# A two-layer trunk with grouped experts: scattered rows inside the weight stream, three experts by selection, modulation on TensorE, and another order around the overflow loop

## Chip, cores and metric

One core of a Trainium2 chip. The metric is the time of one execution in device microseconds (us); lower is better. "Before" is the median of three runs.

## What is computed

A trunk of two layers over 512 tokens of width 1024, all in float32. Each layer takes a modulation from a condition vector, mixes tokens (layer 0 with a chunkwise matrix memory, layer 1 with differential attention), then routes every token to 2 of 16 experts of one group. Cut to what matters:

```python
for l in range(2):
    mod = silu(c) @ w_ada[l] + b_ada[l]                # 1024 -> 6 * 1024
    sh1, sc1, g1, sh2, sc2, g2 = split(mod, 6)
    h = rms(x, norm1[l]) * (1 + sc1) + sh1
    x = x + g1 * mixer[l](h)                           # layer 0: mLSTM, layer 1: attention
    h = rms(x, norm2[l]) * (1 + sc2) + sh2
    # every token: its best group of 4 experts, the best 2 in it, normed weights
    y = sum over its 2 experts of weight * ((silu(h @ w_gate) * (h @ w_up)) @ w_down)
    x = x + g2 * y
```

## The kernel before

**Start.** `load` (lines 209 to 216) asks for a chunk on SP's queue. `ada_half` (272 to 296) makes half of shift and scale of layer 0: for each of the two, two chunks of 4 x 128 rows by 512 columns; ScalarE and VectorE multiply each row block by its scalar of silu(c) and add them up in `acc`; `column_sums` (259 to 265) turns the result with TensorE and reduces it on VectorE. `modulated` (359 to 364) then makes the operand of the first projection, `proj_cols` (424 to 437). The second half, `rest_of_h` (491 to 496), runs between the first products. All products of the large matrices are triples: a weight is split by `split` (218 to 223) into a high part (ScalarE) and a low part (VectorE, for some POOL), and `triple` (225 to 230) multiplies high by high, low by high, high by low.

**Routing.** `route` (974 to 1176) gives `tile_done` (1009): per 128 tokens, POOL multiplies the token rows, ScalarE takes the square sum, `rstd_of` (317) makes the root on POOL; `logits` (1032), `choose` (1046) and `place` (1071) follow with tiny VectorE instructions. `order` (1107) ranks the 13 experts of varying size by their counts and finds how many blocks overflow (`past`); `by_rank` (1137) sorts row numbers and weights by rank; `weigh` (1152) makes the weights. Then `overflow` (1455 to 1476), a loop over overflow blocks with a count known only at run time: every engine reads `past` and passes the loop's entry and exit.

**Experts.** `moe` (1239 to 1577) takes 16 experts in turn: 9 with 128 tokens in triples, the last 7 (`few`) with 64 tokens in plain float32, TensorE holding 64 columns of tokens, the weights moving, two halves side by side. An expert is 6 parts of 1 MB: 4 gate-up, 2 down. `sequence` (1207) gives their order, `Prefetch` (1227) asks for them into 15 buffers, each as an earlier part is used up. Results go back in two ways. Most experts write theirs, weighted, with an indirect transfer into a table of 1024 rows in memory (`keep`, `keep_few`, 1312). The last two (`NSEL`) are added by selection: a 0/1 matrix (`places`, 1322) multiplies the weighted result (`weighted_few`, 1306) into the 512 tokens (`to_tokens`, 1329); their table rows are filled with zero rows at expert 1. Near the end `scattered_rows` (1478 to 1490) reads the table back in eight transfers of 512 KB into buffers of the splits, and `combine` (1492 to 1497) adds the two rows of each token, multiplies by the modulation row and adds to the tokens: three VectorE instructions per 128 tokens. `keep_in_program_order` (`ordered`) fixes the order of these instructions, and TensorE's of the last experts, as written; a scheduler sets the rest.

In the last expert: `combine((0,))` ahead of the activation, (1, 2) behind it, (3) behind the down product; then the selection products and an addition for each half of each 128 tokens, and in layer 1 the transfers out.

## Time and profile before

| | |
|---|---|
| median of 3 runs | 1259.03 us (1256.88 to 1259.57) |
| profiled execution, its own time | 1258.35 us |
| its span, first to last instruction | 1256.4 us |
| TensorE busy, share | 1113.8 us, 89% |
| VectorE, ScalarE, POOL busy | 70%, 56%, 30% |
| mean granted TensorE clock | 0.932 |
| moved | 320.79 MB, mean 255 GB/s |

Times in the rows count from the span's start. A busy share is an average over stages of different kinds: layer 0 has its mixer up to about 250 us, routing to 320, experts to 590; layer 1 its mixer to 950, routing to 978, experts to the end. PE is TensorE, DVE VectorE, ACT ScalarE, POOL GpSimd, SP the engine that asks for transfers. "[x <-y]" behind a row is the idle time of its engine before it and what ended that. The granted clock is 1.00 at 2.4 GHz and 0.50 at 1.2 GHz.

### The profile page before, as it was taken

What the parts mean: (1) busy time and instruction counts of PE and PEld (TensorE: products, weight loads), DVE (VectorE), ACT (ScalarE), POOL (GpSimd) and SP (SyncE); (2) the same over time, 40 slices, a digit from 0 to 9 for tenths busy, and PEclk for the clock granted to TensorE, in tenths of its full rate; (3) what the DMA queues carried; (4) which work ended last, traced back from release to release, by engine and by line L of the source; (5) the groups of instructions that cost most, each with busy time, mean ns of one, the idle gap of its engine ahead of it and who ended that gap; (6) DMA issues with size and microseconds to landing.
All of it is one profiled execution on the core that took longest, in us unless ns stands there. A gap on an engine that the chain in (4) does not pass through costs nothing. (4 is left out here: it accounts for less than half of the span.)

```text
span 1256.4 us, 16914 instructions
## 1 busy us (share of the span) xinstructions
PE 1113.8 (89%) x5714; PEld 816.6 (65%) x5714; DVE 873.6 (70%) x1622; ACT 698.2 (56%) x1164; POOL 381.4 (30%) x273
## 2 busy tenths in 40 slices
PE   3899999987899999995799999888897999999994
PEld 2577877766777875332688877665576787875331
DVE  6955878887788994006767889795776798993006
ACT  5456675442788884112656666565552788884110
POOL 2544572452211111102351455551332211101100
PEclk7799999997899999998799999897896899999997
DMA  9777662183899999998233335320464799999995
GB/s 349 248 246 282 243 233 101 66 341 143 289 390 383 377 390 365 397 409 272 94 102 117 119 127 175 131 73 1 168 248 167 268 386 375 387 384 366 391 410 202
DMA packets 105196, 320.79 MB, mean 255 GB/s; under 512 B 12674, under 2 KB 25098, under 8 KB 105105
## 3 DMA queue, kind: packets, MB, share of 16 engines
q1 hardware_dynamic: 96272, 298.67, 64.6%
q0 software_dynamic: 8832, 20.99, 4.6%
q8 instruction: 47, 0.77, 0.2%
q14 instruction: 45, 0.36, 0.1%
HBM read 309.66 MB, written 20.45 MB: 263 GB/s over the span
## 5 line engine op out<-in xcount | busy, mean ns | idle before, releaser
L253 POOL TENSOR_TENSOR acc<-acc,ada 128x1024 f32<-128x1024 f32 x58 | 151.0, 2604 | 89.4 <-ACT ada L252 36.7
L1275 PE MATMUL pge<-we,xfe 128*64 128x512 f32 x448 | 103.2, 599 | 2.5 <-DMA we<-in_moe_w_gu_dram 2.5
L1247 POOL DMA_INDIRECT xg<-h2d,lstd x26 | 26.4, 1016 | 235.8 <-PE xTe L380 156.3
L1284 DVE TENSOR_TENSOR acte<-acte,pge 128x256 f32<-128x256 f32 x14 | 5.9, 420 | 125.0 <-ACT acte L1283 125.0
L252 ACT ACTIVATE ada<-ada,cact 128x1024 f32<-128x1024 f32 x58 | 64.7, 1143 | 30.8 <-DMA ada<-in_w_ada_dram 30.7
L1275 PEld LDWEIGHTS pge<-we,xfe 128*64 128x64 f32 x448 | 29.3, 136 | 55.6 <-issue 48.2
L877 ACT ACTIVATE p<-p,mx 128x128 f32<-128x128 f32 (+3 forms) x64 | 35.6, 557 | 42.5 <-DVE mx L876 42.5
L1302 PE MATMUL pye<-we,aTe 128*64 128x512 f32 x224 | 54.1, 624 | 1.7 <-ACT aTe L1291 1.1
L320 POOL TENSOR_TENSOR qrs<-qrs,nhalf 128x4 f32<-128x4 f32 x32 | 36.7, 1151 | 61.2 <-DVE qrs L319 47.8
L870 PE MATMUL s<-kTb,qTb 64*128 64x128 f32 (+3 forms) x128 | 44.8, 530 | 11.1 <-DVE mx L873 10.4
L465 POOL TENSOR_TENSOR wo<-wo,grow 128x1024 f32<-128x1024 f32 x16 | 40.1, 2523 | 30.2 <-DVE wos102l L222 15.1
L1302 PEld LDWEIGHTS pye<-we,aTe 128*64 128x64 f32 x224 | 16.4, 144 | 36.5 <-issue 31.9
L873 DVE CUSTOM_DVE_ANT_0 p<-s,maskW 128x128 f32<-128x128 f32 (+3 forms) x64 | 29.8, 484 | 12.6 <-PE s L870 5.5
L1283 ACT ACTIVATE acte<-pge 128x256 f32<-128x256 f32 x14 | 5.4, 384 | 54.6 <-PE pge L1275 54.6
L1333 PE MATMUL pcf<-yo,self 64*128 64x512 f32 x64 | 18.9, 636 | 17.6 <-DVE acte L1284 15.9
L1314 ACT ACTIVATE yo<-pye,twins 128x512 f32<-128x512 f32 x10 | 6.9, 687 | 48.7 <-PE pye L1302 48.7
L1315 POOL DMA_INDIRECT yd<-yo,rows x10 | 10.0, 998 | 78.1 <-ACT yo L1314 77.5
L844 DVE TENSOR_TENSOR qrow<-qrow,qrs 128x256 f32<-128x256 f32 x32 | 26.5, 828 | 7.9 <-POOL qrs L320 7.6
L1291 ACT ACTIVATE aTe<-aTe 128x256 f32<-128x256 f32 x14 | 5.4, 383 | 45.5 <-PE aTe L1289 45.5
L1398 POOL DMA_INDIRECT yd<-yoe,lstd x12 | 14.7, 1225 | 52.4 <-ACT yoe L1503 50.7
L320 POOL TENSOR_TENSOR ors<-ors,nhalf 128x2 f32<-128x2 f32 (+1 forms) x12 | 12.0, 999 | 58.9 <-DVE ors L319 25.0
L250 DVE SCALAR_TENSOR_TENSOR acc<-ada,cact,acc 128x1024 f32<-128x1024 f32 x12 | 15.4, 1281 | 19.4 <-POOL acc L253 16.5
(2545 smaller groups left out, 3963.2 us busy)
## 6 DMA issues: line engine op xcount, KB each, us to landing
we<-in_moe_w_gu_dram SPq DMA_DIRECT2D x128, 1024.0 KB, 9.4
we<-in_moe_w_down_dram SPq DMA_DIRECT2D x64, 1024.0 KB, 10.5
ada<-in_w_ada_dram SPq DMA_DIRECT2D x48, 1024.0 KB, 5.2
yk<-yd SPq DMA_DIRECT2D x16, 512.0 KB, 10.0
wo<-in_a_w_out_dram SPq DMA_DIRECT2D x4, 1024.0 KB, 4.9
wo<-in_b_w_out_dram SPq DMA_DIRECT2D x4, 1024.0 KB, 6.2
x<-in_x_dram SPq DMA_DIRECT2D x4, 512.0 KB, 5.2
qk0w<-in_a_w_in_dram SPq DMA_DIRECT2D x2, 1024.0 KB
```

The costliest lines, as they stand in the source:

```text
L252: A.activation(raw[:, k], raw[:, k], AF.Copy, scale=cact[:, kt:kt + 1])
L253: G.tensor_tensor(acc, acc, raw[:, k], op=ALU.add)
L320: G.tensor_tensor(r, r, nhalf[:, 0:ncol], op=ALU.pow)
L465: G.tensor_tensor(raw[:, k], raw[:, k], grow, op=ALU.mult)
L844: V.tensor_tensor(row3, row3, r[:, :, None].to_broadcast([P, ng, BHD]), op=ALU.mult)
L870: T.matmul(ps[:, 0:n], part(qTs, h)[q0:q0 + BHD, j * P:(j + 1) * P], part(kTs, h)[q0:q0 + BHD, 0:n], start=True, stop=True)
L873: V.tensor_tensor_reduce(p[:, 0:n], ps[:, 0:n], maskW[:, S - n:S], scale=1.0, scalar=NEG, op0=ALU.add, op1=ALU.max, accum_out=mx[:, cc:cc ...
L877: A.activation(p[:, 0:n], p[:, 0:n], AF.Exp, scale=0.125, bias=mx[:, cc:cc + 1], accum_out=mx[:, 2 + cc:3 + cc])
L1247: G.indirect_dma_start(out=xg[0:n], out_offset=None, in_=h2d[:, :], in_offset=bass.IndirectOffsetOnAxis(ap=itok[0:n], axis=0), bounds_chec ...
L1275: T.matmul(pgu[hf * CS:(hf + 1) * CS].rearrange("p (g c) -> p g c", g=2), x[:, kt], w[:, :, hf], start=kt == 0, stop=kt == NK - 1))
L1302: T.matmul(py[hf * CS:(hf + 1) * CS], aT[:, k, ch * CS:(ch + 1) * CS], w[:, 0, hf * 512:(hf + 1) * 512], start=ch + k == 0, stop=ch + k == 2))
L1333: ordered(T.matmul(banks[hf], sel[at, t], yo[at], start=first, stop=last))
```

## The change

- `ada_half`: TensorE multiplies. silu(c) is laid into `cpad`, 32 columns of which only the first is not zero; four products per chunk write to four quarters of a bank, over 512 columns; the bank is copied to a row, and eight products with a column of ones per half sum over the partitions.
- `tile_done`: the square sum and the root come first in program order; POOL's root of a tile is put between the two halves of its product.
- `by_rank`, the making of `ids` and the last addition to the weights move behind the overflow loop. The first expert's first two weight splits move ahead of the loop.
- The loop's body is rewritten with plain float32 products (fewer instructions).
- `NSEL` is 3: three experts are added by selection, three lists get zero rows.
- The table is read back in four transfers of 1 MB that are parts of the weight stream, ahead of gate-up parts 2 and 3 and both down parts of the last expert, into weight buffers; parts from there on are held back until the last scatter has been asked for. `combine` of tokens 0 and 1 stands at the last expert but one, 2 ahead of the last activation, 3 behind it.

The diff, cut to its core (the loop's body is left out):

```diff
-NSEL = 2
+NSEL = 3
...
+    cpad = wsp.tile([P, NK, 32], F32, tag="wlo", name="cpad", bufs=N_LO)
+    V.memset(cpad, 0.0)
+    V.tensor_copy(cpad[:, :, 0], cact)
...
     def ada_half(hf, where):
-        accs = []
+        rows = []
         for i, j in enumerate((1, 0)):
-            acc = room[0].tile([P, D], F32, tag="acc", name=f"acc0{j}{hf}", bufs=2)
-            accs.append(acc)
+            ps = (y_tile, t_tile)[hf](f"rowada{j}{hf}")
             for ch in range(2):
                 raw = load(...)
-                c = [cact[:, ch * 4 + k:ch * 4 + k + 1] for k in range(4)]
-                for n in range(2):
-                    A.activation(raw[:, n] if ch else acc[:, n * 512:(n + 1) * 512], raw[:, n], AF.Copy, scale=c[n])
-                if ch:
-                    V.tensor_tensor(acc, acc, raw[:, 0:2].rearrange("p a n -> p (a n)"), op=ALU.add)
-                for n in range(2):
-                    part = acc[:, n * 512:(n + 1) * 512]
-                    V.scalar_tensor_tensor(part, raw[:, 2 + n], c[2 + n], part, op0=ALU.mult, op1=ALU.add)
-            V.tensor_tensor(acc[:, 0:512], acc[:, 0:512], acc[:, 512:], op=ALU.add)
+                for k in range(4):
+                    T.matmul(ps[k * 32:(k + 1) * 32], cpad[:, ch * 4 + k], raw[:, k], start=ch == 0, stop=ch == 1)
+            row = room[0].tile([P, 512], F32, tag="acc", name=f"row0{j}{hf}", bufs=2)
+            if i:
+                A.activation(row, ps, AF.Copy)
+            else:
+                V.tensor_copy(row, ps)
+            rows.append(row)
         def sums():
-            column_sums(cs, accs[::-1], f"psada0{hf}")
+            ps = t_tile(f"psada0{hf}")
+            for i, row in enumerate(rows[::-1]):
+                for k in range(4):
+                    T.matmul(ps[:, i * 4 + k:i * 4 + k + 1], row[:, k * P:(k + 1) * P], ones_f[:, 0:1], start=True,
+                             stop=True)
...
         def tile_done(t):
+            A.activation(xT.rearrange("p k t -> p (k t)"), xt[t], AF.Square, accum_out=ss)
+            before = pows[-1:]
+            rst[t] = rstd_of(ss, 1, D, f"re{l}{t}", pows)
             for n in range(2):
-                G.tensor_tensor(h2[:, cols], xt[t][:, cols], arow[:, cols], op=ALU.mult)
-            A.activation(xT.rearrange("p k t -> p (k t)"), xt[t], AF.Square, accum_out=ss)
-            rst[t] = rstd_of(ss, 1, D, f"re{l}{t}")
+                with tc.issue_after((pows[-1] if n else before[0]).ins) if n or before else nullcontext():
+                    G.tensor_tensor(h2[:, cols], xt[t][:, cols], arow[:, cols], op=ALU.mult)
...
         def order():
-            later(1, lambda: by_rank(perm, work[:, 2 * N2:5 * N2]))
...
-        def by_rank(perm, moved):
+        def by_rank(work):
+            V.tensor_tensor(sg, sg, held[0], op=ALU.add)
...
+            V.tensor_tensor(perm, rk[:, None, :].to_broadcast(square), eidx[:, 0:ND, None].to_broadcast(square),
+                            op=ALU.is_equal)
+            V.tensor_tensor(turned, perm[0:1], eidx[0:1, None, dyn].to_broadcast([1, ND, ND]), op=ALU.mult)
+            V.tensor_reduce(idf, turned, axis=AX.X, op=ALU.add)
+            V.tensor_copy(ids, idf)
...
         def weigh(q, sc, oh, tmp, hot):
-                V.tensor_tensor(sg, sg, psg, op=ALU.add)
+                held.append(psg)
...
     def sequence(l, ids):
         for e in range(NE):
+            if e == NE - 1:
+                yield from (yds[l][t * 2 * P:(t + 1) * 2 * P, :].rearrange("(p k) d -> p k d", k=2) for t in range(NT))
             yield from (gu(e, 2), gu(e, 3))
...
     class Prefetch:
+            self.first_row, self.owed, self.free = 6 * (NE - 1) + 2, 0, False
         def more(self, n=1, after=None):
             for part in islice(self.parts, n):
-                self.ready.append(load(part, 2, D, f"we{self.n}", self.slots[self.n % len(self.slots)], after))
+                held = self.n >= self.first_row
+                last[:] = loads[-1:] if held else last
+                raw = load(part, 2, D, f"we{self.n}", self.slots[self.n % len(self.slots)], after)
+                (self.rows if held and self.n < self.first_row + NT else self.ready).append(raw)
+                last[:] = loads[-1:] if held else last
+        def step(self, n=1):
+            self.owed += n
+            n = self.owed if self.free else min(self.owed, self.first_row - self.n)
+            self.owed -= n
+            self.more(n)
...
         def combine(ts):
             for t in ts:
-                ordered(V.tensor_tensor(yks[t, 0], yks[t, 0], yks[t, 1], op=ALU.add))
+                yk = fetch.rows[t]
+                ordered(V.tensor_tensor(yk[:, 0], yk[:, 0], yk[:, 1], op=ALU.add))
...
         rows_in(0)
+        ready = [split(fetch.ready[0][:, k:k + 1], 1, D, f"guse0{k}") for k in range(2)]
         overflow()
...
         rows_in(1)
+        by_rank(yo_tile("work"))
         gate_up(cur, weights, (0, 1), "e0")
...
             if not nxt:
                 mine = places(e)
-                combine((0,))
+                combine((2,))
             act, done = activate_few(cur, nm) if few else (activate(cur, nm), None)
+            if e >= NE - 2:
+                ordered(done)
+                combine((0, 1) if nxt else (3,))
             if not nxt:
-                ordered(done)
-                scattered_rows((2, 3))
-                combine((1, 2))
                 for t in range(2):
-                    to_tokens(banks[t], t, *before_last, True, False)
+                    for i, chosen in enumerate(selected):
+                        to_tokens(banks[t], t, *chosen, i == 0, False)
...
                 mine = weighted_few(py, e), mine
-                combine((3,))
...
-            elif e == NE - 2:
-                before_last = weighted_few(py, e), places(e)
-            elif e == NE - 3:
-                def keep_and_load(py=py, e=e):
-                    keep_few(py, e)
-                    scattered_rows((0, 1))
-                late.append(keep_and_load)
+            elif e >= NE - NSEL:
+                selected.append((weighted_few(py, e), places(e)))
+            elif e == NE - NSEL - 1:
+                keep_few(py, e)
+                fetch.free = True
+                fetch.step(0)
```


## Rows read from the trace of the kernel before

**Rows 1.** The page, 40 equal slices: busy tenths of TensorE, transfers' busy share in tenths
```profile
PE   3899999987899999995799999888897999999994
DMA  9777662183899999998233335320464799999995
```

**Rows 2.** Windows: stretch, length, busy us (instructions) by engine, granted clock, DMA share, GB/s
```profile
15.00:30.00 15.00, 1.97 (x8) 1.57 (x8) 12.43 (x15) 7.02 (x10) 5.16 (x2) 0.53 1.05 387
1000.00:1050.00 50.00, 50.00 (x228) 39.88 (x227) 44.94 (x45) 42.64 (x51) 10.65 (x9) 1.00 1.01 381
```

**Rows 3.** Timeline of the start: start us, us, engine, line, operation, out<-in, count [idle before]
```profile
20.98 1.33 ACT L283 ACTIVATE ada<-ada,cact 128x512 f32<-128x512 f32 x2 [1.36 <-DMA ada<-in_w_ada_dram]
31.72 0.15 DVE L295 TENSOR_TENSOR mod<-cs,vcol 128x8 f32<-128x8 f32 x1
33.58 2.08 PE L432 MATMUL qk0p<-ah,qk0s0h 128*128 128x512 f32 x4 [3.77 <-ACT ah L356]
40.25 1.06 ACT L221 ACTIVATE qk0s4h<-qk0w 128x1024 fp32r<-128x1024 f32 x1 [1.56 <-DMA qk0w<-in_a_w_in_dram]
57.02 0.63 PE L433 MATMUL qk0p<-al,qk0s4h 128*128 128x512 f32 x1
```

**Rows 4.** Timeline of the routing of layer 1: last root and last logits
```profile
954.26 3.23 PE L1037 MATMUL psr<-awr,x2T 128*128 128x16 f32 x16
954.93 0.55 POOL L320 TENSOR_TENSOR re<-re,nhalf 128x1 f32<-128x1 f32 x1 [0.62 <-DVE rt L1159]
```

**Rows 5.** Timeline of layer 1 around the loop
```profile
969.14 0.17 DVE L1174 TENSOR_TENSOR cols<-cols,psg 128x16 f32<-128x16 f32 x1 [1.98 <-PE psg L1170]
970.80 0.61 PE L1148 MATMUL twins<-byrank,twin 64*128 64x21 f32 x2 [1.70 <-DVE byrank L1143]
971.71 0.06 DVE L1457 MEMSET trip<- 128x1 f32 x1
975.33 1.23 DVE L222 TENSOR_TENSOR guse00l<-we,guse00h 128x1024 fp32r<-128x1024 f32 x1 [3.55 <-ACT guse00h L221]
975.37 1.97 PE L380 MATMUL xTe<-ident,xg 128*128 128x128 f32 x8 [3.95 <-ACT guse00h L221]
977.73 0.80 PE L230 MATMUL pge<-guse00h,xh0e 128*128 128x512 f32 x1 [0.39 <-ACT xh0e L382]
```

**Rows 6.** Timeline of layer 0 around the loop, and a line of its body asked for
```profile
313.10 0.06 DVE L1457 MEMSET trip<- 128x1 f32 x1
319.48 0.79 PE L230 MATMUL pge<-guse00h,xh0e 128*128 128x512 f32 x1 [1.85 <-ACT xh0e L382]
nothing on L1476; most used: ['L230', 'L407', 'L408', 'L409', 'L1275', 'L215', 'L222', 'L221', 'L1302', 'L380', 'L902', 'L1037', 'L870', 'L1261', 'L264', 'L1460', 'L892', 'L1380', 'L856', 'L873', 'L330', 'L432', 'L313', 'L1025', 'L877']
```

**Rows 7.** Timeline of the last expert and the end of layer 1
```profile
1220.23 1.94 PE L1275 MATMUL pge<-we,xfe 128*64 128x512 f32 x8 [0.62 <-DMA we<-in_moe_w_gu_dram]
1222.79 1.94 PE L1275 MATMUL pge<-we,xfe 128*64 128x512 f32 x8 [0.62 <-DMA we<-in_moe_w_gu_dram]
1230.47 1.23 DVE L1495 TENSOR_TENSOR yk<-yk,yk 128x1024 f32<-128x1024 f32 x1 [10.00 <-DMA yk<-yd]
1234.13 0.41 DVE L1284 TENSOR_TENSOR acte<-acte,pge 128x256 f32<-128x256 f32 x1
1243.27 0.75 DVE L1308 SCALAR_TENSOR_TENSOR yo<-pye,twins,grow 128x512 f32<-128x512 f32 x1 [1.42 <-PE pye L1302]
1244.07 5.42 PE L1333 MATMUL pcf<-yo,self 64*128 64x512 f32 x24 [0.86 <-DVE yo L1308]
1249.30 3.07 DVE L1558 TENSOR_TENSOR x<-x,pcf 128x512 f32<-128x512 f32 x5
```

**Rows 8.** Timeline of the end of layer 0's experts and the first split of layer 1
```profile
584.93 0.75 DVE L1308 SCALAR_TENSOR_TENSOR yo<-pye,twins,grow 128x512 f32<-128x512 f32 x1 [0.98 <-PE pye L1302]
587.66 1.06 ACT L221 ACTIVATE b00s0h<-b00w 128x1024 fp32r<-128x1024 f32 x1 [7.80 <-DVE x L1558]
595.68 1.29 DVE L1558 TENSOR_TENSOR x<-x,pcf 128x512 f32<-128x512 f32 x2
```

More of the change, by code (lines that the diff above doesn't have):

```diff
@@ L1322, in places @@
         def places(e):
-            sel = pool.tile([P, NT, P], F32, tag=f"xl{e % 2}", name=f"self{e}")
+            where, tag = (small, "sel") if e == NE - 1 else (pool, f"xl{e % 2}")
+            sel = where.tile([P, NT, P], F32, tag=tag, name=f"self{e}", bufs=1)
             for t in range(NT):
@@ L1356, in gate_up @@
                     kt = ch * 2 + k
-                    hi, lo = split(raw(k), 1, D, f"gus{nm}{kt}")
+                    hi, lo = ready.pop(0) if ready else split(raw(k), 1, D, f"gus{nm}{kt}")
                     triple(pg, pu, *xs[kt], hi, lo, kt == 0, kt == NK - 1)
@@ new lines, in product @@
+                def product(ps, xs, w):
+                    for kt, x in enumerate(xs):
+                        raw = part(w, kt)
+                        for n in range(2):
+                            T.matmul(ps[n], x, raw[:, n * 512:(n + 1) * 512], start=kt == 0, stop=kt == len(xs) - 1)
+                    return ps
+                xs = turned(xgs[1][:, 0:512], "xh0") + turned(xgs[1][:, 512:], "xh1")
+                act = activate((None, *product([mm_tile("pgo"), mm_tile("puo")], xs, moe_w_gu)), "o")
@@ new lines, in overflow @@
+                py = product([y_tile("py0o"), y_tile("py1o")], turned(act, "ahi"), moe_w_down)
+                gate, token = place
+                sel = small.tile([P, NT, P], F32, tag="sel", name="selo", bufs=1)
+                yo = yo_tile("o")
+                for n in range(2):
+                    V.scalar_tensor_tensor(yo[:, n * 512:(n + 1) * 512], py[n], gate, grow[:, n * 512:(n + 1) * 512],
+                                           op0=ALU.mult, op1=ALU.mult)
+                for t in range(NT):
+                    V.tensor_scalar(sel[:, t], slot, float(t * P), token, op0=ALU.add, op1=ALU.is_equal)
+                    for n in range(2):
+                        ps = t_tile(f"pco{t}{n}")
+                        T.matmul(ps, sel[:, t], yo[:, n * 512:(n + 1) * 512], start=True, stop=True)
+                        x = xt[t][:, n * 512:(n + 1) * 512]
+                        V.tensor_tensor(x, x, ps, op=ALU.add)
```

94 lines of the change are left out of this document (32 added, 62 removed).

## The prediction

> **What bounds the kernel now.** I read four views in this order. First the slices of the page: TensorE is at most half busy in slices 1, 19 and 40 and not full in 10, 20 and 31, and busy nearly throughout between them; the transfers are near their full rate in the start and in both expert phases (12 to 18, 33 to 39) [rows 1]. So time can be won where TensorE stands still: at the start, at the two routings, at the two ends of the expert phases. Then the stretches by window: from 15 to 30 us TensorE worked 1.97 us at a granted clock of 0.53 while transfers ran at 387 GB/s; from 1000 to 1050 us it worked all 50 us at 1.00 [rows 2]. Then the timeline of each of these places. The start is held by VectorE's arithmetic on the modulation [rows 3]; the routing by a loop that every engine has to pass together [rows 4 to 6]; the end by transfers and by VectorE's order [rows 7, 8].
>
> **A, modulation by TensorE.** Before, the last of four chunks of the first half is taken up at 20.98 us, the modulation is ready at 31.72, the first projection product starts at 33.58 [rows 3]; TensorE has nothing else to do meanwhile. After, each chunk is four products with 32 columns of stationary data, 512 moving columns, into four quarters of one bank. No row has this form. The nearest is the 64-wide pair: eight instructions (four products in two pairs) in 1.94 us, 0.97 us a pair at full clock [rows 7]. If four overlap as two do, a chunk costs 0.97, or 1.94 at the 1.2 GHz level that this stretch has [rows 2]. Behind the last chunk: 1.94 (products) + 0.75 (copy of 128x512, by the like instruction in [rows 8]) + 3.23 (16 instructions of column sums, by the 16 narrow ones in [rows 4]) + 0.15 (the add, [rows 3]) + 1.86 (31.72 to 33.58, unchanged) = 7.9 us; at 2.4 GHz 5.6. First product at 26.6 to 28.9; I take 28.3, a gain of 5.3.
>
> The second half decides what remains. Before, the second strip's split starts at 40.25, but its products run on from 57.02 only [rows 3], since the second modulation ends late. By then TensorE has done 48 products of the first strip, 4 of the second and some 10 of the gates. At 50.00/228 = 0.22 us each [rows 2] these are 13.6 us. After: 28.3 + 13.6 + 5 (four chunks, between 3.9 and 7.8) + 2.5 (column sums) + 2.5 (products still at the low clock) = 51.9, against 57.02 plus about 1.7 us that the products from 57.02 on lose, since they begin at the low clock (0.63 us long, [rows 3]). A = -6.9, say **-7.0**. The strip is split by about 45 us, and TensorE reaches it at about 48: this covers its transfer; without the cover 3 us return. VectorE and ScalarE lose their work of this part, which nobody then waits for. Ends: -10 (all at full clock, sums of the first row already done) and a loss, if the narrow products do not overlap (rival 1).
>
> No row has narrow products beside full ones. The Trainium skill (TensorEngine Tiling (Array Packing), section Tiling Modes) says that changing the tiling mode drains TensorE; the page has no time for it. [...]
>
> **B, routing and loop.** The loop's body leaves no instruction in the trace [rows 6]; only its passage costs. Before it, VectorE works from 969.14 to 971.77 on the sums by rank and TensorE on their product at 970.80; then the engines leave the loop, TensorE's first transposes come at 975.37 and the first product at 977.73 [rows 5]. After, the work by rank stands behind the loop. The last arrival is then TensorE's share product (before 969.1) or VectorE with two early splits (1.23 us each, [rows 5]) if they stand last: 969.1 to 969.6 instead of 971.4 to 971.8, 2.2 to 2.7 less; four small rank instructions that leave VectorE's queue ahead of the loop give up to 0.9 more. Behind the loop, the transposes take 1.97 for two halves, and the product waits for ScalarE's copy of the first half; this copy no longer queues behind the splits: 0.6 less. Together 2.9 to 4.2; I take 3.6. About 3 us of rank work then stands in VectorE's queue behind the loop, with the expert splits and the low parts of the tokens behind it; it is covered by the transposes and by two splits made early. Without the cover 3 us return. SP's next weight address waits for the same work, but that part is asked for only after the first products. Layer 0 has the same interval, from 313.10 to 319.48 [rows 6]. From the first product on TensorE is busy throughout [rows 2, 5], so the gain moves all that follows. B = 2 x -3.6 = **-7.2**, ends -1 and -8.4.
>
> The new order on POOL (root between the two halves of a tile's product) I cost at nothing: before, the last root starts at 954.93 and takes 0.55, but the scores wait for TensorE's logits, 954.26 to 957.49 [rows 4]. If POOL were late, it has 2 us to spare.
>
> **C and D, the ends.** Before, scattered rows are asked for behind all weights; VectorE waits 10.00 us for them, until 1230.47, and has three instructions to do before the last expert's activation (1234.13); the result is taken up at 1243.27, selection products 1244.07 to 1249.49, last add 1252.37 [rows 7]. After, 4 MB of rows lie ahead of the last four weight parts. The three additions of each tile (3 x 1.23) lie beside transfers, and the activation waits for the last gate-up part. That part is the 15th MB where the first rows were the 14th: a part takes 2.56 us (1220.23 to 1222.79), so it lands between 1230.5 and 1233.0; I take 1231.7. Plus 2.4 (its products, partly at the low clock) and 0.9: activation ready at 1235.0, before 1234.54. From there to the result before took 8.7 us, much of it at a low clock, since TensorE had stood still; now it has just worked, and four more selection instructions (0.23 each) stand ahead: 7.0. Result 1242.0, 1.2 earlier. Behind it 32 selection instructions instead of 24: 7.2 + 0.75 + 0.9 = 8.9 against 9.1, where VectorE still had additions. D = **-1.4** (ends -4 and +3).
>
> In layer 0 the same chain, but from result to last add 12.0 us (584.93 to 596.97), because the additions meet the next layer's splits, which themselves waited for buffers until 587.66 [rows 8]. The new rows lie in weight buffers, so those splits go ahead. -1.2 and 12.0 - 8.9 = 3.1: C = **-4.3** (ends 0 and -7).
>
> The third selected expert costs one scatter less and one zero scatter more per layer, POOL work of about 1 us each that nobody waits for. SP now waits for the scatter of the expert before, and the last four weight parts are queued behind that wait; several parts of 2.56 us each are then under way, so nothing runs dry. If this cover failed, the last weights would come as much later as that scatter lands.
>
> **Sum** against the profiled execution, 1258.35 us (span 1256.4): -7.0 - 7.2 - 4.3 - 1.4 = -19.9, 1238.5. The median of the runs is 0.7 higher: **1239 us**.
>
> **Rivals.** 1. *Narrow products run one after another.* For it: no row has four in one bank. Against: pairs overlap. Alone and at the low clock a chunk is 7.8 us where chunks come every 2.7; four chunks end at about 44, the first product starts near 50 instead of 33.6, and the second half puts up to 15 us between the products, part of it into the old gap. A = +24, total 1270: slower. It decides from A = +13, that is from half that price. Chance 0.06.
> 2. *Strict order of transfers, and the ends give back.* The last gate-up part lands at 1233.0 or later, its products run at the low clock, and the additional selection products come on top: C = -1, D = +2, total 1246. For it: parts land in the order of issue, 2.56 us apart [rows 7]. Against: TensorE's clock afterwards. Chance 0.14. The Trainium skill (DMA: Bandwidth & Descriptors, section Queues, rings and completion order) says that each DMA engine takes descriptors in ring order, which this trace bears out and which speaks for this rival.
> 3. *The rank work only changes its place*: it blocks VectorE behind the loop, B = -1: total 1245. Chance 0.08.
> 4. *The start is held by transfers anyway* and the others only half come: within 0.2% (about what a measurement of this kernel can tell from no change). Chance 0.03.
>
> **How the numbers follow.** My forecast, all four terms within their ends, has 0.69; its own range is 1229 to 1247. Rivals 2 and 3 (0.22) lie at 1245 and 1246, with doubt to 1251. Range 1229 to 1251. Faster 0.90, same 0.03, slower 0.07.
>
> **What would show it.** Right: first projection product before 30 us, TensorE's clock not falling again at 52 to 56; six us from loop entry to first product becoming about four; no wait for rows at the end, VectorE's additions done before the last result. Wrong: narrow products of over 2 us a chunk; a wait of VectorE's splits behind rank work; the last down parts landing after TensorE is ready for them.

## The result and the profile after

The changed kernel takes 1245.06 us (median of 5 runs, 1244.41 to 1250.01), the kernel before 1259.03 us in the runs beside it: a ratio of 0.9906 (95%: 0.988 to 0.9933). Its profiled execution took 1244.82 us with a span of 1243.0, so the trace has to explain 13.5 us where the forecast had 19.9. The gain is 0.9%, clear of no change. The time lies in the forecast's range of 1229 to 1251, 6 us above the forecast of 1239, and within 1 us of the totals of rival 2 (1246) and rival 3 (1245). By the total alone these two would look better than the forecast; only the stages can decide.

I set the same marks in both traces and took differences. (a) and (d) are the first of the last additions to x ahead of a routing, (b) and (e) the first expert product, (c) the first b00p product of layer 1.

| mark | before | after | so far | this stage | forecast for the stage |
|---|---|---|---|---|---|
| (a) layer 0, x ready | 289.61 | 282.17 | -7.4 | -7.4 (A) | -7.0 |
| (b) layer 0, first expert product | 319.48 | 308.66 | -10.8 | -3.4 (B) | -3.6 |
| (c) layer 1, first b00p product | 605.71 | 591.30 | -14.4 | -3.6 (C) | -4.3 |
| (d) layer 1, x ready | 948.02 | 936.74 | -11.3 | **+3.1** (attention) | 0 |
| (e) layer 1, first expert product | 977.73 | 962.40 | -15.3 | -4.0 (B) | -3.6 |
| end of the span | 1256.4 | 1243.0 | -13.4 | **+1.9** (D) | -1.4 |

Four stages came within 0.7 us (C by another step than the forecast one, as is shown below). The miss is in two: the attention of layer 1, which the change does not edit, and the last end.

The start, timeline of after (start us, us, engine, line, operation, out<-in, count [idle before <-what ended it]):

```profile
20.98 1.07 PE L285 MATMUL rowada<-ada,cpad 128*32 128x512 f32 x8 [1.55 <-DMA ada<-in_w_ada_dram]
26.49 1.94 PE L285 MATMUL rowada<-ada,cpad 128*32 128x512 f32 x8 [0.19 <-DMA ada<-in_w_ada_dram]
28.68 1.65 PE L438 MATMUL qk0p<-ah,qk0s0h 128*128 128x512 f32 x3 [0.25 <-ACT ah L362]
...
34.26 0.40 PE L438 MATMUL qk0p<-ah,qk0s0h 128*128 128x512 f32 x1
34.58 1.06 PE L285 MATMUL rowada<-ada,cpad 128*32 128x512 f32 x8
35.58 0.50 PE L439 MATMUL qk0p<-al,qk0s0h 128*128 128x512 f32 x1
35.92 0.39 PE L440 MATMUL qk0p<-ah,qk0s0l 128*128 128x512 f32 x1
...
51.07 0.50 PE L439 MATMUL qk0p<-al,qk0s4h 128*128 128x512 f32 x1
```

A chunk of narrow products takes 1.07 us at a granted clock of 1.00, and 1.94 at 0.50. The first projection product starts at 28.68 instead of 33.58, and the second strip's products run on from 51.07, where before they ran on from 57.02 only [rows 3]. The clock does not fall there any more. Windows of before (stretch, length, busy us (instructions) of PE, PEld, DVE, ACT, POOL, granted clock, DMA share, GB/s) and of after:

```profile
52.00:62.00 10.00, 7.28 (x20) 5.40 (x21) 9.96 (x13) 4.38 (x6) 8.62 (x15) 0.66 0.67 178
```
```profile
50.00:62.00 12.00, 12.00 (x52) 9.08 (x52) 11.73 (x20) 5.45 (x8) 7.04 (x7) 1.00 0.52 149
...
1198.00:1211.00 13.00, 6.05 (x26) 1.61 (x26) 5.64 (x5) 0.38 (x1) 0.00 (x0) 0.86 1.02 418
1211.00:1223.00 12.00, 7.66 (x22) 2.41 (x24) 6.47 (x8) 0.39 (x1) 0.00 (x0) 0.59 0.73 293
```

The last two belong to the end of layer 1: transfers are at their full rate up to 1211, and TensorE, which waits for them, falls to a granted clock of 0.59. The timeline of that end in after, the queue's issues (SPq) first:

```profile
1187.60 6.18 SPq L218 DMA_DIRECT2D we<-yd  x4
1195.23 2.94 SPq L218 DMA_DIRECT2D we<-in_moe_w_gu_dram  x2
...
1205.25 1.23 DVE L1509 TENSOR_TENSOR we<-we 128x1024 f32<-128x1024 f32 x1 [8.15 <-DMA we<-yd]
1215.34 6.40 PE L1298 MATMUL pge<-we,xfe 128*64 128x512 f32 x16 [10.62 <-DMA we<-in_moe_w_gu_dram]
1229.98 0.75 DVE L1331 SCALAR_TENSOR_TENSOR yo<-pye,twins,grow 128x512 f32<-128x512 f32 x1 [3.69 <-PE pye L1325]
1230.79 7.14 PE L1357 MATMUL pcf<-yo,self 64*128 64x512 f32 x32 [0.86 <-DVE yo L1331]
1237.96 1.28 DVE L1575 TENSOR_TENSOR x<-x,pcf 128x512 f32<-128x512 f32 x2 [1.29 <-PE pcf L1357]
```

VectorE still waits for rows, 8.15 us instead of 10.00 [rows 7], but this wait ends at 1205.25 and holds up nothing: its additions are done before the last result. What holds the end now is a wait of TensorE, 10.62 us, for the gate-up parts that are issued behind the rows. The routing of layer 1 in after:

```profile
936.74 1.88 DVE L459 TENSOR_TENSOR x<-x,po 128x512 f32<-128x512 f32 x3 [0.57 <-PE po L233]
938.54 1.33 DVE L225 TENSOR_TENSOR guse01l<-we,guse01h 128x1024 fp32r<-128x1024 f32 x1
939.80 0.67 DVE L459 TENSOR_TENSOR x<-x,po 128x512 f32<-128x512 f32 x1
...
956.23 1.86 PE L1179 MATMUL psg<-shares,hot 128*128 128x16 f32 x8 [1.60 <-DVE past L1135]
962.40 0.80 PE L233 MATMUL pge<-guse00h,xh0e 128*128 128x512 f32 x1
```

From the share product to the first expert product 6.2 us pass. But one of the early splits stands between the third and the fourth of the last additions to x, which now end 3.73 us after the first begins (before 2.48).

### The profile page after: what moved, and what is told of

The parts are those of the page before. It is cut to its first block, busy times and chain, and to the rows that moved or that the text cites. A ratio compares the mean times of both kernels' runs of the same rounds, so it can differ in the third digit from the quotient of the medians.

```text
span 1243.0 us, 17100 instructions
## 1 busy us (share of the span) xinstructions
PE 1128.2 (91%) x5826; PEld 824.4 (66%) x5826; DVE 855.2 (69%) x1608; ACT 686.7 (55%) x1146; POOL 378.7 (30%) x273
## 4 chain that ended last, share of the span: by engine, by line
PE 63%; DVE 18%; DMA 10%; ACT 3%; issue 2%; POOL 2%; SPq 0%; DVEq 0%; POOLq 0%; ACTq 0%
PE pge L233 8%; PE pue L233 8%; PE pge L1298 7%; PE po L233 6%; PE py0e L233 4%; DMA ada<-in_w_ada_dram 4%; PE py1e L233 4%; DMA we<-in_moe_w_gu_dram 3%; PE pye L1325 3%; PE s L876 2%; DMA b00w<-in_b_w_in_dram 2%; PE xTe L386 1%; PE o L908 1%; DVE qrow L856 1%; PE pcf L1357 1%
## 5 line engine op out<-in xcount | busy, mean ns | idle before, releaser
L1298 PE MATMUL pge<-we,xfe 128*64 128x512 f32 x448 | 106.9, 619 | 19.3 <-DMA we<-in_moe_w_gu_dram 19.3
L1270 POOL DMA_INDIRECT xg<-h2d,lstd x26 | 26.5, 1018 | 225.1 <-PE xTe L386 154.5
L1325 PE MATMUL pye<-we,aTe 128*64 128x512 f32 x224 | 50.8, 594 | 1.7 <-ACT aTe L1314 1.1
L471 POOL TENSOR_TENSOR wo<-wo,grow 128x1024 f32<-128x1024 f32 x16 | 40.1, 2524 | 29.7 <-DVE wos102l L225 14.9
L879 DVE CUSTOM_DVE_ANT_0 p<-s,maskW 128x128 f32<-128x128 f32 (+3 forms) x64 | 29.8, 485 | 10.1 <-PE s L876 7.2
L326 POOL TENSOR_TENSOR ors<-ors,nhalf 128x2 f32<-128x2 f32 (+1 forms) x12 | 11.9, 998 | 56.3 <-DVE ors L325 28.2
L908 PE MATMUL o<-vb,aTs 128*128 128x128 f32 x160 | 27.2, 308 | 1.5 <-ACT o L937 0.8
L386 PE MATMUL xTe<-ident,xg 128*128 128x128 f32 x144 | 23.0, 290 | 5.8 <-POOL we L216 3.3
L908 PEld LDWEIGHTS o<-vb,aTs 128*128 128x128 f32 x160 | 23.8, 217 | 6.2 <-ACT aTs L900 1.9
L876 PEld LDWEIGHTS s<-kTb,qTb 64*128 64x128 f32 x128 | 16.0, 203 | 16.2 <-DVE mx L879 8.6
```

The source lines that it names most:

```text
L326: pows.append(G.tensor_tensor(r, r, nhalf[:, 0:ncol], op=ALU.pow))
L386: T.transpose(ps[:, k * P:(k + 1) * P], row[:, kt * P:(kt + 1) * P], ident)
L471: G.tensor_tensor(raw[:, k], raw[:, k], grow, op=ALU.mult)
L876: T.matmul(ps[:, 0:n], part(qTs, h)[q0:q0 + BHD, j * P:(j + 1) * P], part(kTs, h)[q0:q0 + BHD, 0:n], start=True, stop=True)
L879: V.tensor_tensor_reduce(p[:, 0:n], ps[:, 0:n], maskW[:, S - n:S], scale=1.0, scalar=NEG, op0=ALU.add, op1=ALU.max, accum_out=mx[:, cc:cc ...
L908: T.matmul(po[:, 0:P], aT[:, kb * P:(kb + 1) * P], part(vs, h)[:, kb * P:(kb + 1) * P], start=kb == 0, stop=kb == j)
```

## The experiments

All stages in us, from the profiled execution of each kernel, so that no experiment's gain is read from the total alone. (a) to (e) are the marks above; the last column is the median with the ratio to before.

| kernel | start to a | a to b | b to c | c to d | d to e | e to end | median, ratio (95%) |
|---|---|---|---|---|---|---|---|
| before | 289.6 | 29.9 | 286.2 | 342.3 | 29.7 | 278.7 | 1259.03 |
| after | 282.2 | 26.5 | 282.6 | 345.4 | 25.7 | 280.6 | 1245.06, 0.9906 (0.988 to 0.9933) |
| e1 | 288.8 | 26.4 | 282.4 | 337.2 | 26.4 | 280.2 | 1247.43, 0.9907 (0.9889 to 0.9925) |
| e2 | 281.9 | 29.3 | 285.3 | 341.4 | 29.3 | 279.8 | 1249.63, 0.9928 (0.9904 to 0.9951) |
| e3 | 303.0 | 27.8 | 281.8 | 344.0 | 26.0 | 279.8 | 1264.61, 1.0053 (1.0026 to 1.008) |
| e4 | 281.8 | 27.2 | 279.5 | 336.7 | 25.9 | 276.6 | 1231.83, 0.9782 (0.9765 to 0.9799) |
| e5 | 282.5 | 29.8 | 283.5 | 340.5 | 28.4 | 278.8 | 1245.43, 0.9892 (0.9873 to 0.9912) |
| e6 | 281.2 | 32.5 | 284.9 | 342.2 | 31.7 | 280.9 | 1255.3, 0.9976 (0.9955 to 0.9997) |
| e7 | 282.1 | 26.1 | 281.5 | 335.0 | 25.7 | 276.5 | 1230.73, 0.979 (0.9759 to 0.9822) |
| e8 | 284.7 | 33.3 | 281.6 | 337.6 | 33.0 | 277.5 | 1246.05, 0.9881 (0.9849 to 0.9912) |
| e9 | 280.6 | 27.4 | 282.4 | 349.4 | 25.8 | 281.4 | 1246.48, 0.9882 (0.9836 to 0.9927) |
| e10 | 280.4 | 26.2 | 277.7 | 343.4 | 25.9 | 277.4 | 1231.89, 0.9794 (0.9759 to 0.983) |
| e11 | 281.7 | 26.4 | 280.6 | 337.9 | 26.2 | 273.8 | 1228.3, 0.976 (0.9733 to 0.9788) |
| e12 | 281.8 | 28.2 | 285.7 | 342.7 | 27.7 | 280.2 | 1247.46, 0.9892 (0.9854 to 0.9929) |

### A: the modulation (e1, e2, e3)

**e1**: the changed kernel with the modulation of before.

```diff
-                for k in range(4):
-                    T.matmul(ps[k * 32:(k + 1) * 32], cpad[:, ch * 4 + k], raw[:, k], start=ch == 0, stop=ch == 1)
+                for n in range(2):
+                    A.activation(raw[:, n] if ch else acc[:, n * 512:(n + 1) * 512], raw[:, n], AF.Copy, scale=c[n])
...
```

> After, with the modulation's first quarter computed on ScalarE and VectorE again as before; all else as after. Theory: part A is worth 6 to 7 us up to the first routing, and the 3 us that layer 1's attention lost against before (347 to 348.5 us from the first b00p product to the last addition to x, before 344.1) come from another order of instructions that the planner chose there; in this kernel that order is again nearly that of before. So: first projection product at 33.6, first expert product of layer 0 at 315, attention 344 to 345.5, total 1247 to 1249. Rival: the attention's loss is a matter of clock and alignment with no tie to the order: attention 347 or more, total 1251 to 1252.

**e2**: the kernel before, with the new modulation alone (the lines of the diff from `cpad` to `sums`).

> Before, with the modulation's first quarter on TensorE alone. Theory: first projection product at 28.7 instead of 33.6, second strip at 50 to 51 instead of 57, first expert product of layer 0 at 313.3 (319.5 before), attention as before at 344, end as before: total 1251.5 to 1252.5. Rival: the start's gain is given back in the first mixer or at the ends, whose transfers do not move: total 1255 or more.

**e3**: the changed kernel with all narrow products of a half in one quarter, where they cannot overlap; the same sums.

```diff
-                    T.matmul(ps[k * 32:(k + 1) * 32], cpad[:, ch * 4 + k], raw[:, k], start=ch == 0, stop=ch == 1)
+                    T.matmul(ps[0:32], cpad[:, ch * 4 + k], raw[:, k], start=ch == 0 and k == 0,
+                             stop=ch == 1 and k == 3)
...
```

> After, with the four narrow products of a chunk all into the same quarter of the bank, one behind the other, instead of into four quarters; the same sums. Theory: the four quarters overlap, and alone each product costs what the four together cost, so a chunk takes 3.9 to 4.3 us at the full clock instead of 1.07; the first projection product comes at 35 to 37 instead of 28.7, the second strip 12 to 18 us later than after's 51, total 1255 to 1263. Rival: narrow products are short by themselves and quarters matter little: a chunk under 1.5 us, total within 1 us of after.

At mark (a) the modulation is worth 6.6 us in the changed kernel (e1) and 7.7 in the kernel before (e2); the forecast had 7.0. At the end the two differ more: e2 is 9.4 us shorter in both median and profile, e1 only 2.4 slower than after by the medians and 1.5 shorter in the profile, because its attention took 8 us less. So e2's total came 2 us below what was expected of it, and e1's attention, counted as in its expectation, took 340.3 us, which neither the theory (344 to 345.5) nor the rival (347 or more) had. That pointed to the attention as a thing of its own. The timeline of e3 shows what the overlap is worth:

```profile
13.05 13.92 PE L285 MATMUL rowada<-ada,cpad 128*32 128x512 f32 x32
...
36.51 1.20 PE L439 MATMUL qk0p<-ah,qk0s0h 128*128 128x512 f32 x4
```

Four chunks in one quarter take 13.92 us, 3.48 a chunk (expected 3.9 to 4.3) against 1.07 in four quarters, both at a granted clock of 1.00. Mark (a) comes 20.8 us later than in the changed kernel and 13.4 later than in the kernel before, and the kernel is slower than before. So rival 1 priced the lack of overlap too high (+24, with a low clock that e3 did not have), but it would have decided the sign; the overlap rules it out. Rival 4 is out as well, since the start did move.

### D and C: where the rows stand (e4, e7, e10, e11)

**e4**: the rows go between the last expert's gate-up parts and its down parts, and are added behind the activation.

```diff
         for e in range(NE):
+            yield from (gu(e, 2), gu(e, 3))
             if e == NE - 1:
                 yield from (yds[l][t * 2 * P:(t + 1) * 2 * P, :].rearrange("(p k) d -> p k d", k=2) for t in range(NT))
-            yield from (gu(e, 2), gu(e, 3))
...
-            self.first_row, self.owed, self.free = 6 * (NE - 1) + 2, 0, False
+            self.first_row, self.owed, self.free = 6 * (NE - 1) + 4, 0, False
...
-            if e >= NE - 2:
+            if not nxt:
                 ordered(done)
-                combine((0, 1) if nxt else (3,))
+                combine(range(NT))
```

> After, with the scattered rows read between the last expert's second gate-up half and its down parts, and VectorE's additions of them behind the last expert's activation. Theory: at both ends TensorE stood still for 8.7 to 13 us until the last gate-up parts landed, and the chain behind them (activation, turn, down products, results) ran after the last transfer; now only the down products and the results stand behind it: layer 1's end 4 to 5 us shorter, layer 0's end 3 to 4 us shorter, attention 344 to 345.5 by the order that the planner chose: total 1232 to 1237. Rival: the ends are held by the sum of transfers and by VectorE's additions (12 of 1.23 us), which now come later: no gain at the ends, total 1241 to 1246.

The end of layer 1 in e4, timeline:

```profile
1194.17 1.94 PE L1298 MATMUL pge<-we,xfe 128*64 128x512 f32 x8 [0.63 <-DMA we<-in_moe_w_gu_dram]
1196.69 1.94 PE L1298 MATMUL pge<-we,xfe 128*64 128x512 f32 x8 [0.59 <-DMA we<-in_moe_w_gu_dram]
1198.56 3.70 PE L1357 MATMUL pcf<-yo,self 64*128 64x512 f32 x16
1209.29 5.30 PE L1325 MATMUL pye<-we,aTe 128*64 128x512 f32 x16 [6.65 <-DMA we<-in_moe_w_down_dram]
```

The gate-up parts come 2.5 us apart, with some 0.6 us of waiting for each, and the long wait is now one for the down parts, 6.65 us instead of 10.62. From (e) to the end 276.6 us, 4.0 less than after; from (b) to (c) 3.1 less. The medians differ by 13.2, more than these 7.1: 8.8 us of the profiled gain lie in the attention (339.7 us counted as in the expectation, which had 344 to 345.5).

**e7**: two selected experts instead of three.

```diff
-NSEL = 3
+NSEL = 2
```

> After, with two experts by selection instead of three; the rows are still read ahead of the last expert's second gate-up half, but can be asked for only when the scatter one expert (11.6 us) later has landed. Planned order of the attention as before. Theory: some 20 us of parts are under way when the rows are held (issue to landing 20 us), so the transfers do not run dry or only for a few us, while 8 selection products less save 1.5 us at each end; attention 340 to 344: total 1235 to 1240. Rival: the held parts leave the transfers idle, each end 3 to 6 us longer: 1242 to 1250.

```profile
1202.36 6.55 PE L1298 MATMUL pge<-we,xfe 128*64 128x512 f32 x16 [10.61 <-DMA we<-in_moe_w_gu_dram]
1208.84 2.14 PE L1357 MATMUL pcf<-yo,self 64*128 64x512 f32 x8
1216.38 5.42 PE L1357 MATMUL pcf<-yo,self 64*128 64x512 f32 x24 [0.86 <-DVE yo L1331]
```

The wait for the gate-up parts is the same 10.61 us, although the rows wait for a later scatter and are asked for 10.2 us later behind (e), so the scatter on which they wait held nothing up; the third selection costs 1.56 us ahead of the down products (3.70 against 2.14) and 1.72 behind the result (7.14 against 5.42). Layer 1's end is 4.1 us shorter with two, layer 0's 1.1; the rest of the 4.1 lies ahead of the wait. The median is 4 us below what was expected, partly because the attention was short again.

**e10**: as e4, but the rows of tiles 2 and 3 behind the down parts, and their additions beside the last selection products.

```diff
             if e == NE - 1:
+                yield from (rows(t) for t in (0, 1))
...
             yield from (dn(e, 0), dn(e, 1))
+        yield from (rows(t) for t in (2, 3))
```

> The kernel with all rows between the last expert's gate-up and down parts (1231.8), with the rows of the last two token tiles moved behind the down parts and their additions beside the last selection products. Planned order of the attention: nearly after's (0.97 alike on VectorE, 0.69 to before's). Theory: the down parts land 5 us earlier, the results with them, and VectorE's additions for the last two tiles end 4 to 5 us behind the last transfer: each end 3 to 5 us shorter than with all rows between (layer 1 from the first expert product to the last addition 271.5 there), but the attention 345 to 349 instead of 339.7: total 1229 to 1234. Rival: VectorE's additions behind the last landing hold the end, no gain there: 1236 to 1241.

Against e4 it gains 1.8 us at the end of layer 0 and loses 0.8 at the end of layer 1, where 3 to 5 less had been expected. TensorE's wait for a down part falls to 1.69 us there, but then VectorE holds the end: it works without a pause from 1214.68 on, and from the result to the last add 14.5 us pass instead of 9.3. That is the rival of the expectation. The medians are alike (1231.89, 1231.83).

**e11**: e4 and e7 together.

> The kernel with all rows between gate-up and down, with two experts by selection instead of three. Theory: 8 selection products less behind each layer's last result, 1.7 us each, and the rows are asked for some 5 us later without the transfers running dry; the planner's order of the attention is a third one (0.68 like before's, 0.52 like after's), so its length is open between 338 and 349: ends 3 us shorter in sum, total 1228.5 where the attention keeps 339.7, up to 1238 where it takes 348.5. Rival: the later rows delay the down parts, the ends 2 to 4 us longer each.

1228.3 us, 1.3% below the changed kernel and 2.4% below the kernel before; from (e) to the end 273.8 us, 6.8 less than after and 2.8 less than e4. Its interval overlaps those of e4 and e7, so that it beats both kernels is measured, that it beats e4 and e7 is not.

### B: routing and loop (e5, e6, e8, e9, e12)

**e5**: the work by rank ahead of the loop again.

```diff
+        by_rank(yo_tile("work"))
         overflow()
...
         rows_in(1)
-        by_rank(yo_tile("work"))
```

> After, with the work by rank ahead of the loop again; all else as after (its early splits, rows in the weight stream, third selection). Its planned order of layer 1's attention is that of before. Theory: the work by rank ahead of the loop costs 2.2 to 2.7 us at each routing, from the last addition to x to the first expert product (after 23.4 and 22.6 us), and the attention takes 340 to 344 us where after's order took 348.5: total 1241 to 1246, with both effects to be read apart in the trace. Rival: what was gained at the routings came from the early splits and the short instructions, and the place of the rank work matters little: routings as after's within 0.7 us, total 1236 to 1240.

From the copy that sets `past` to the first product: 11.06 and 10.70 us before, 7.15 and 6.38 after (layers 0 and 1), 9.63 and 9.10 in e5. The place of the work by rank is worth 2.5 and 2.7 us, most of B, so rival 3 is out. e5's median is all the same like that of the changed kernel, since its attention took 4.9 us less.

**e6**: the second early split's low part is held behind `past`, to keep it out of the additions to x. **e8**: the same in e4.

```diff
-        on.tensor_tensor(lo, raw, hi.bitcast(F32), op=ALU.subtract)
+        with tc.issue_after(after.ins) if after else nullcontext():
+            on.tensor_tensor(lo, raw, hi.bitcast(F32), op=ALU.subtract)
...
-        ready = [split(fetch.ready[0][:, k:k + 1], 1, D, f"guse0{k}") for k in range(2)]
+        ready = []
+        for k in range(2):
+            ready.append(split(fetch.ready[0][:, k:k + 1], 1, D, f"guse0{k}", after=pows[-1] if k else None))
```

> After, with the second early low part on VectorE issued behind the test of the loop's bound instead of among the last additions to x. Theory: in after it stood between the third and the last addition to x (last addition 3.06 us behind the first, before 1.81), so 1.2 us return at each routing, and VectorE has 2 us of waiting behind the bound to hide it; the attention keeps after's kind of order, 346.5 to 348.5: total 1241 to 1243. Rival: VectorE is then the last to reach the loop, or the copy and the product that follow wait for it: no gain, 1244 to 1246.

> The kernel with the rows between gate-up and down (1231.8) and with the second early low part behind the test of the loop's bound. Theory: 1.2 us less at each routing, nothing else changes: 1228.5 to 1230.5. Rival: no gain, 1231 to 1233.

The additions took 2.48 us again, as meant, but each routing became 6 to 7 us longer, which neither expectation had. The timeline of e6, the issue first:

```profile
961.68 0.38 SPq L218 DMA_DIRECT2D we<-in_moe_w_gu_dram  x1
...
960.56 1.86 PE L1180 MATMUL psg<-shares,hot 128*128 128x16 f32 x8 [1.60 <-DVE past L1136]
970.62 1.97 PE L387 MATMUL xTe<-ident,xg 128*128 128x128 f32 x8 [8.20 <-SPq L1462]
```

The two splits free the buffer of the first weight part. With the second one late, the part that goes into that buffer is issued at 961.68, right ahead of the loop, and the loop lets no engine pass until it has landed: from 962 to 969.3 SP's queue moved 1.05 MB, this part, and then the engines pass. The waits of e6 (engine, line <- what it waited for: us in total, times, longest):

```profile
SPq L1462 <- SPq L1462: 7.0, 1, 7.0
```

**e9**: the line with the early splits taken out. **e12**: that, and the loop's body of before.

```diff
-        ready = [split(fetch.ready[0][:, k:k + 1], 1, D, f"guse0{k}") for k in range(2)]
+        ready = []
```

> After, without the two early splits: the first expert's first two splits stand behind the loop as before. The planned order of layer 1's attention is after's, instruction for instruction on VectorE. Theory: the last addition to x comes 1.2 us or more earlier at each routing, and the first product waits 0.6 to 1.6 us longer behind the loop, so the early splits are worth next to nothing: total 1243 to 1246; attention 347 to 348.5 us by the order. Rival: the early splits carry the routing's gain, 2 us or more each: 1248 or more; and for the attention, a length of 338 to 344 would say that the order doesn't decide it.

> After, with the body of the overflow loop as before (its weights and tokens split into high and low parts in the buffers that the first expert's splits use too) and without the two early splits named in the code. Theory: it is the new loop body, not the line that names the early splits, that lets the planner put the first expert's splits ahead of the loop; here they stand behind it again. Then no split stands among the last additions to x (last addition 1.8 us behind the first, after 3.06), and the first product waits for the copy of the tokens behind the splits again, 2 us longer behind the loop: from the first of the last additions to the first expert product 27.0 to 28.5 us in both layers, after 26.5 and 25.7. Attention as in the kernel with the second early part behind the loop's bound, whose order it shares: 340 to 345. Total 1241 to 1246. Rival: the loop's body only costs where it runs; routings as after's within 0.5 us.

In e9 the instructions of TensorE, VectorE, ScalarE and POOL come in the same order as in the changed kernel (but for one small MEMSET at the start), where the expectation had the splits behind the loop: the instruction scheduler puts the splits ahead of the loop by itself. e9 is thus a repeat of it, and shows the spread of one program: its attention took 349.4 us against 345.4, its median is 1.4 us higher. With the old body (e12) the splits stay behind the loop, the additions take 2.48 us, and `past` to first product takes 9.61 and 9.34; from (a) to the first product it is 1.7 and 2.1 us more than after. The body that was rewritten inside the loop is what let work cross it.

## Why the prediction was right, and where it failed

**A** (forecast -7.0, measured -7.4) held by its own steps: first product forecast at 28.3, measured 28.68; second strip running on at 51.9, measured 51.07; column sums 3.23, measured 3.54; a chunk between 0.97 and 1.94, measured 1.07. Among full products a chunk adds little: in the timeline above the full products on both sides of it take 0.32 us (34.26 to 34.58) and 0.34 us (35.58 to 35.92) from start to start instead of 0.22, 0.2 more for both changes together. The Trainium skill (TensorEngine Tiling (Array Packing), section Tiling Modes) says that a change of the tiling mode drains TensorE, without a price; by these rows it costs some 0.1 us a change, and the forecast, which had no term for it, did not need one.

**B** (forecast -3.6 a layer, measured -3.4 and -4.0): the size was right, one step of it was not. I had TensorE's share product or VectorE's splits arrive last at the loop. The waits of after name the gather of the tokens instead, which POOL issues at 955.16 (engine, line <- what it waited for: us in total, times, longest):

```profile
SPq L1461 <- DMA xg<-h2d,lst: 1.3, 1, 1.3
```

So with the rank work gone, the landing of the gather is the next bound at the loop. And the splits, which I had cost only where they might stand last at the loop, stand among the additions to x: these end 1.25 us later in each layer, of which 0.5 and 0.3 us are left at the copy that sets `past`. The new order on POOL was not tested by itself.

**C** (forecast -4.3, measured -3.6): the size nearly came, one of its two steps did not. Counted from (b), the result came 1.5 us earlier (forecast 1.2), though TensorE waits 8.72 us for gate-up parts in layer 0 too. Behind the result I had the last additions to x end 3.1 us sooner, because the next layer's splits would go ahead. They did go ahead, but from the result to the last add's end 12.2 us pass, before 12.0. The timeline of after:

```profile
570.03 1.06 ACT L224 ACTIVATE b00s0h<-b00w 128x1024 fp32r<-128x1024 f32 x1 [1.18 <-DMA b00w<-in_b_w_in_dram]
581.24 1.15 ACT L255 ACTIVATE ada<-ada,cact 128x1024 f32<-128x1024 f32 x1 [2.94 <-DMA ada<-in_w_ada_dram]
...
583.46 0.15 DVE L325 TENSOR_SCALAR r<-ss 128x1 f32<-128x1 f32 x1 [3.78 <-ACT sq L332]
583.54 1.29 DVE L1575 TENSOR_TENSOR x<-x,pcf 128x512 f32<-128x512 f32 x2
```

ScalarE waits for a part of the next modulation, its square sum stands behind that, and the last two additions stand behind VectorE's use of the square sum. What was gained behind the result, 2.1 us in all, lies behind the last add: from its end to the first b00p product 6.5 us pass, before 8.7. So C came near its number partly by luck. From (b) to (c) e1, e3, e5 and e9 took 281.8 to 283.5 us, like after, and e2 285.3, like before; e6 and e12, whose splits stand otherwise at the loop, took 284.9 and 285.7, which stays open.

**D** failed (forecast -1.4, measured +1.9). On the clock of before I had the last gate-up part land at 1231.7, between 1230.5 and 1233.0. Less the 15.3 us that (e) came earlier, that is 1216.4, at most 1217.7; the part is issued at 1197.8 and lands 20.1 us later, at 1217.8, 1.4 later than I took. TensorE's last eight products start at 1218.81 only, since the first part's eight stand ahead of them at a granted clock of 0.59, and end 3.9 us behind the landing, where I had 2.4. From the activation to the result it took 7.35 us (forecast 7.0), from there to the last add's end 9.26 (8.9). Together 3.6 us more than forecast, of which 0.3 came back behind the last add. That is rival 2 at this end (D = +2), not at the other (it had C = -1). What I had weighed against it, TensorE's clock afterwards, did not hold: I had TensorE come to the last products straight from work, and it waits 10.62 us just there, for the same 4 MB that took VectorE's wait off the path. e4 and e7 show both halves: rows behind the gate-up parts give 4.0 us back, one selection less gives 4.1. The +1.9 is one pair of executions: from (e) to the end the seven kernels with this end (after, e1, e3, e5, e6, e9, e12) took 278.8 to 281.4 us, the two with the end of before (before, e2) 278.7 and 279.8. On average that is a loss of 1.0 us, where the forecast had a gain of 1.4. The Trainium skill (DMA: Bandwidth & Descriptors, section Queues, rings and completion order) has each DMA engine take descriptors in ring order; the order of landing here agrees, rows before gate-up parts.

**The attention** (forecast 0, measured +3.1) is the step that the prediction did not have: it let every gain move all that follows at constant length. Layer 1's attention is not edited, but the instruction scheduler ordered it anew (VectorE's order agrees only to 0.69 with that of before). The timeline of after, VectorE with the additions of POOL that run beside it:

```profile
692.71 2.35 DVE L273 TENSOR_TENSOR mod<-cs,vcol 128x8 f32<-128x8 f32 x1
695.23 2.35 DVE L856 TENSOR_TENSOR qrow<-qrow,rot 128x64 f32<-128x64 f32 x1
697.75 2.49 DVE L888 TENSOR_SCALAR p<-p,mx 128x512 f32<-128x512 f32 x1
700.27 2.71 DVE L889 TENSOR_TENSOR p<-p,p 128x512 f32<-128x512 f32 x1
...
691.83 13.36 POOL L256 TENSOR_TENSOR acc<-acc,ada 128x1024 f32<-128x1024 f32 x5 [2.33 <-ACT acc L251]
...
704.91 0.69 PE L862 MATMUL qkT<-ident,qrow 128*128 128x128 f32 x2 [5.67 <-ACT aTs L900]
```

Before, three of these fell between two of POOL's additions, beside a small instruction:

```profile
711.78 0.15 DVE L270 TENSOR_TENSOR mod<-cs,vcol 128x8 f32<-128x8 f32 x1
711.89 0.49 DVE L882 TENSOR_SCALAR p<-p,mx 128x512 f32<-128x512 f32 x1
712.41 0.69 DVE L883 TENSOR_TENSOR p<-p,p 128x512 f32<-128x512 f32 x1
...
709.47 2.37 POOL L253 TENSOR_TENSOR acc<-acc,ada 128x1024 f32<-128x1024 f32 x1 [16.09 <-ACT acc L248]
711.79 1.02 POOL L320 TENSOR_TENSOR qrs<-qrs,nhalf 128x4 f32<-128x4 f32 x1
712.80 7.57 POOL L253 TENSOR_TENSOR acc<-acc,ada 128x1024 f32<-128x1024 f32 x3
```

Beside POOL's additions each takes about as long as one of these, and TensorE waits 5.67 us for what comes of them. The Trainium skill (SBUF — State Buffer, section Who interferes with whom) says that a VectorE instruction with two inputs in SBUF contends with a GpSimd instruction that reads SBUF; the rows agree, 0.15 us against 2.35 for the same 128x8 addition. TensorE's clock falls in that stretch: a window of after, and of before at the same distance from (c) (in the 12 us ahead of each, at 1.00, TensorE had worked 9.25 us in after and all 12 before):

```profile
702.00:709.00 7.00, 4.09 (x19) 3.64 (x20) 3.02 (x12) 5.50 (x12) 3.11 (x2) 0.51 0.69 250
```
```profile
716.40:723.40 7.00, 4.98 (x42) 4.68 (x43) 6.75 (x11) 4.91 (x12) 3.89 (x2) 1.00 0.47 150
```

But the wait itself is not the 3.1 us. The whole stage from (c) to (d), before, after, e9 and e7:

```profile
605.71:948.02 342.31, 302.71 (x1923) 252.80 (x1924) 262.28 (x697) 205.01 (x494) 145.63 (x87) 0.92 0.36 125
```
```profile
591.30:936.74 345.44, 307.51 (x1923) 258.29 (x1924) 266.28 (x697) 207.76 (x496) 145.69 (x87) 0.90 0.35 124
```
```profile
590.40:939.75 349.35, 310.70 (x1923) 261.93 (x1924) 266.38 (x696) 207.97 (x496) 145.94 (x87) 0.89 0.35 122
```
```profile
589.66:924.65 334.99, 297.46 (x1923) 248.93 (x1924) 266.37 (x696) 206.47 (x495) 145.37 (x87) 0.94 0.37 128
```

TensorE stands still 39.6 us of the stage before and 37.9 after: other waits became shorter. What grew is its busy time, by 4.8 us for the same 1923 products, at a lower granted clock.

How much of this is order is only partly settled. The kernels with the order of after took 343.4 to 349.4 us from (c) to (d) (after, e3, e9, e10), with TensorE busy for 306.9 to 310.7 us at granted clocks of 0.89 to 0.91. Those with nearly the order of before took 335.0 to 342.3 (before, e1, e2, e4, e5, e7, e8), with 297.5 to 304.8 busy at 0.92 to 0.94. TensorE's idle time is 34 to 40 us in both groups. So the groups differ by the clock and not by the waits as such; that the new order brings waits behind which the clock falls, as the one above, fits this, but the order was not set by hand to test it alone. Two executions of one program differ by 4 us too (after, e9), 3.2 of them busy time. e6, e11 and e12 have other orders again (342.2, 337.9, 342.7, all at 0.92). So part of the totals of e4, e7 and e11 is not their edit, and the stages at the ends are what they show.

**The signs that I had named.** The first product came before 30 us and the clock stayed up at 52 to 56. From the loop's entry (VectorE's write of `trip`) to the first product it took 4.2 us in layer 1, as forecast, and 5.0 in layer 0 (before 6.0 and 6.4). VectorE's additions were done at 1226.3, before the last result at 1229.98, but its wait for rows was moved and not removed, and no sign asked for TensorE's wait at the end.

## What to carry to other kernels

When a transfer is moved ahead of another on a saturated queue, price the wait that the other one gets, and who stands still in it, before counting the wait that goes away; here the cheaper place was behind the parts that feed the longer chain. Where a scheduler orders the instructions, an edit can also reorder stages that it does not touch, so compare stage by stage between marks, look in each at TensorE's busy time and granted clock beside its waits, and take the spread of a repeated program before believing a few us. The narrow products paid here because their quarters overlap; without it they were a loss (e3).

## What the hardware showed that I had not expected

- Four products of 32 columns in four quarters overlap to 3.3 times their serial rate (1.07 against 3.48 us a chunk, both at a granted clock of 1.00).
- A loop that every engine passes waited here for transfers issued shortly before it: for the gather after (1.3 us on SP), for a weight part of 1 MB in e6 (7.0 us on SP).
- A VectorE addition of 128x8 that takes 0.15 us takes 2.35 beside POOL's 128x1024 additions, and four instructions drawn out like this in a row held TensorE for 5.67 us.
- The same 1923 products of one unedited stage kept TensorE busy for 297.5 us (e7) to 310.7 us (e9), at granted clocks of 0.94 and 0.89.
